# Layer 0 of a two-layer decoder: weight totals, scales, splits and ring loads half a section later, early loads issued by ScalarE, and another order of the last pair

## The chip, the cores and the metric

The kernel runs on one core of a Trainium2 chip. A core has a matrix engine (TensorE, in the profile PE, with its weight loads as PEld), VectorE (DVE), ScalarE (ACT), GpSimd (POOL) and SyncE (SP), which here does nothing but issue DMAs. Each engine works through its own list of instructions in order. The metric is the device time of one execution in microseconds (us); lower is better. Instructions and lines below (L427) are those of the kernel before.

## The reference

Two layers, each x + W_out(mixer(rmsnorm(x)) * silu(z)), on 1024 tokens of width 1024, 16 heads of 64. Layer 0 is forgetting attention, layer 1 a sparse attention that this change does not touch. Layer 0, cut:

```python
def fox_mixer(h, w_in, b_f, w_out):
    proj = h @ w_in
    q, k, v, f, z = jnp.split(proj, [W, 2 * W, 3 * W, 3 * W + N_HEADS], axis=-1)
    log_f = jax.nn.log_sigmoid(f.astype(jnp.float32) + b_f.astype(jnp.float32))
    c = jnp.cumsum(log_f, axis=1).transpose(0, 2, 1)
    for qb in range(S // FOX_BLOCK):
        logits = jnp.einsum('bqhd,bkhd->bhqk', q[:, s0:s1], k[:, :s1]) * scale
        logits = logits + c[:, :, s0:s1, None] - c[:, :, None, :s1]
        logits = jnp.where(tk[None, :] <= tq[:, None], logits, NEG)
        p = jax.nn.softmax(logits, axis=-1)
        outs.append(jnp.einsum('bhqk,bkhd->bqhd', p, v[:, :s1]))
    return (o * jax.nn.silu(z)) @ w_out
```

## The kernel before

Layer 0 works in 8 pairs of heads. For a pair, four **sections** are projected: k, v, q and z, 32 sections in all, each 128 columns of the weight. A section is two halves of 512 tokens, and a half is 8 steps over the width of 3 matmuls (L267 to L269): the weight and the activations are each split into two f16 parts, high and low, and three products of the parts are added.

A section's weight comes in as f32 by a DMA into a ring of 7 slots (`issue`, L413, tiles `wst_k`, `wst_v`, `wst_q`, `wst_z`). Before it is split, it is scaled by a power of two that is found from the sum of squares of the weight. For this `ring_square` (L421) squares it on ScalarE, five sections ahead, and adds up each row. Once a pair, when the squares of the next pair's four sections are there, `ring_total` casts the four row sums (`wtb`, L425, ScalarE) and adds them over the partitions with one matmul against ones (`wsum`, L427, PE). `ring_scale` (L436 to L441, VectorE) makes the scales from it in `wu`. Then `split_sec` splits the section: the high part on VectorE (L140, `whi_k` and so on), the low part on POOL (L144 and L145, `wlo_k` and so on), which overwrites the slot; a new ring load into that slot has to wait for it.

Between these sections the attention of earlier pairs runs, in units called **duos**: two tiles of 128 queries of one head. A duo's scores are matmuls S (L872 and L873); VectorE adds the bias and finds the minimum `m` (L881); ScalarE takes the exponential (L890) and a copy to f16 (`hl`, L891); VectorE makes the low part (L892); SP issues a DMA that transposes both parts (`pT`, L893); and PE multiplies by v (O, L905 to L907), two duos later. The bias needs `B`, a row of the cumulated forget gates that a DMA spreads over the partitions, and `Bd`, its diagonal block, made on POOL (L861).

A generator for the duos and one for the sections are merged by the planned cost of their matmuls, so that the program of PE alternates between them. What stands where on the other engines follows from the place at which a generator emits it. Each section calls `tick` twice: the first call behind its first half, the second behind its second. `next_w` keeps two split weights ready: called at a section's start, it emits the split of the section after it.

`early` squares further weights ahead of their use: rows of layer 0's output weight and 21 pieces of layer 1's input weight, 29 of up to 512 KB in all, one a section, by a load (L168) and a square on ScalarE (L174). `late_on` keeps an instruction at its place in program order. In the last pair the items are k, v, q, z, while the projections come as z half 1, q half 1, z half 0, q half 0, with a part of the output's work in between.

## Time and profile before

| | |
|---|---|
| median of 3 runs | 1470.51 us (1468.88 to 1470.97) |
| the profiled execution | 1472.43 us |
| its span on the core | 1470.7 us |
| PE busy | 1347.9 us (92%), 11084 matmuls |
| DVE, ACT, POOL busy | 1115.9, 933.7, 645.0 us |
| DMA | 234.79 MB, mean 160 GB/s |
| layer 0 | from about 40 to 600 us |

The profile is that of one execution; its own time is the span and what lies around it. Its second part shows the span in 40 slices of 36.8 us, in tenths, so the layer of interest is slices 2 to 16:

```profile
PE   5979989989998999999999988979999999998998
PEld 3435545555555555444545544446666666665643
DVE  6566677777777798496757666878998999889934
ACT  6666676776767674155455475657877878778512
POOL 0343546355454542221203456245765766755500
```

PE is the engine that is busy nearly throughout. A row of a timeline begins with its start and its duration in us; a bracket at the end tells how long the engine had been idle and what ended that. A view of waits tells who waited for whom, how long in all, how many times, and the longest.

### The profile page before, as it was taken

What the parts mean: (1) busy time and instruction counts of PE and PEld (TensorE: products, weight loads), DVE (VectorE), ACT (ScalarE), POOL (GpSimd) and SP (SyncE); (2) the same over time, 40 slices, a digit from 0 to 9 for tenths busy, and PEclk for the clock granted to TensorE, in tenths of its full rate; (3) what the DMA queues carried; (4) which work ended last, traced back from release to release, by engine and by line L of the source; (5) the groups of instructions that cost most, each with busy time, mean ns of one, the idle gap of its engine ahead of it and who ended that gap; (6) DMA issues with size and microseconds to landing.
All of it is one profiled execution on the core that took longest, in us unless ns stands there. A gap on an engine that the chain in (4) does not pass through costs nothing. (4 is left out here: it accounts for less than half of the span.)

```text
span 1470.7 us, 31545 instructions
## 1 busy us (share of the span) xinstructions
PE 1347.9 (92%) x11084; PEld 792.4 (54%) x11084; DVE 1115.9 (76%) x3005; ACT 933.7 (63%) x2291; POOL 645.0 (44%) x904
## 2 busy tenths in 40 slices
PE   5979989989998999999999988979999999998998
PEld 3435545555555555444545544446666666665643
DVE  6566677777777798496757666878998999889934
ACT  6666676776767674155455475657877878778512
POOL 0343546355454542221203456245765766755500
PEclk9999999999999999999999999999999999999999
DMA  7469789897798997446564547555667777776534
GB/s 271 105 155 196 178 158 219 169 202 189 172 213 174 200 203 178 107 155 201 154 206 125 151 111 161 123 145 89 127 144 155 146 170 128 143 156 147 107 108 143
DMA packets 410895, 234.79 MB, mean 160 GB/s; under 512 B 334000, under 2 KB 372208, under 8 KB 410736
## 3 DMA queue, kind: packets, MB, share of 16 engines
q1 hardware_dynamic: 410736, 232.78, 66.8%
q8 instruction: 87, 1.43, 0.4%
q14 instruction: 72, 0.59, 0.1%
HBM read 120.31 MB, written 28.38 MB: 101 GB/s over the span
## 5 line engine op out<-in xcount | busy, mean ns | idle before, releaser
L890 ACT ACTIVATE P<-P,m 128x512 f32<-128x512 f32 (+1 forms) x192 | 116.4, 607 | 111.6 <-DVE m L881 111.1
L1765 PE MATMUL S_n<-nk,nq 128*128 128x320 f16 (+5 forms) x768 | 154.5, 314 | 14.9 <-DVE m_n L1773 12.4
L1780 POOL TENSOR_TENSOR hl_n<-P_n,hl_n 128x640 f16<-128x640 f32 (+4 forms) x128 | 144.0, 1125 | 9.9
L892 DVE SCALAR_TENSOR_TENSOR hl<-P,hl 128x512 f16<-128x512 f32 (+1 forms) x192 | 120.6, 642 | 28.0 <-ACT hl L891 26.1
L861 POOL TENSOR_TENSOR Bd<-B,tri 128x128 f32<-128x128 f32 x128 | 65.2, 525 | 161.8 <-DVE m L881 129.8
L1779 POOL CAST hl_n<-P_n 128x640 f16<-128x640 f32 (+4 forms) x128 | 75.7, 592 | 125.8 <-ACT P_n L1776 107.2
L1776 ACT ACTIVATE P_n<-P_n,m_n 128x640 f32<-128x640 f32 (+7 forms) x128 | 98.6, 771 | 31.7 <-DVE m_n L1773 31.2
L1776 ACT ACTIVATE P_n<-P_n,m_n,units 128x640 f32<-128x640 f32 (+4 forms) x128 | 100.1, 782 | 21.6 <-DVE m_n L1775 20.3
L284 ACT ACTIVATE pth_n<-ptp_n 128x512 f16<-128x512 f32 (+1 forms) x160 | 85.1, 545 | 41.8 <-PE ptp_n L1798 41.3
L285 DVE SCALAR_TENSOR_TENSOR ptl_n<-ptp_n,pth_n 128x512 f16<-128x512 f32 (+1 forms) x160 | 99.6, 632 | 9.5 <-ACT pth_n L284 7.6
L1765 PEld LDWEIGHTS <-nq 128*128 128x128 f16 x768 | 71.5, 98 | 61.0 <-issue 25.7
L1798 PE MATMUL ptp_n<-ident,P_n 128*128 128x128 f32 x576 | 93.2, 280 | 8.0 <-DVE ptl_n L285 2.4
L891 ACT ACTIVATE hl<-P 128x512 f16<-128x512 f32 (+1 forms) x192 | 92.1, 512 | 6.0 <-DMA pT<-hl 4.1
L1773 DVE CUSTOM_DVE_ANT_0 P_n<-S_n,wmask 128x640 f32<-128x640 f32 (+4 forms) x128 | 83.2, 650 | 7.4 <-PE S_n L1765 6.9
L1798 PEld LDWEIGHTS ptp_n<-ident,P_n 128*128 128x128 f32 x576 | 65.3, 141 | 33.6 <-DVE ptl_n L285 7.1
L872 PE MATMUL S<-KH,Q 128*128 128x512 f32 (+1 forms) x192 | 76.5, 413 | 4.9 <-DVE wu L441 1.9
L97 ACT ACTIVATE h_n<-xr 128x512 f32<-128x512 f32 x32 | 20.0, 625 | 83.3 <-DVE xr L1898 41.0
L1806 PE MATMUL O_n<-nv,pth_n 128*128 128x64 f16 x576 | 71.7, 194 | 1.0 <-ACT pth_n L284 0.6
L1807 PE MATMUL O_n<-nv,pth_n 128*128 128x64 f16 x576 | 71.8, 193 | 0.0
L1773 DVE CUSTOM_DVE_ANT_0 P_n<-S_n,bias,units 128x640 f32<-128x640 f32 (+1 forms) x64 | 68.8, 1075 | 3.0 <-PE S_n L1765 2.9
L905 PE MATMUL O<-v,pT 128*128 128x64 f16 x576 | 59.6, 196 | 10.8 <-DMA pT<-hl 10.8
L1808 PE MATMUL O_n<-nv,ptl_n 128*128 128x64 f16 x576 | 68.8, 193 | 0.6 <-DVE ptl_n L285 0.6
(549 smaller groups left out, 4760.6 us busy)
## 6 DMA issues: line engine op xcount, KB each, us to landing
sq<-in_nsa_w_dram SPq DMA_DIRECT2D x28, 512.0 KB
B<-cD SPq DMA_DIRECT2D x16, 512.0 KB
nq<-qD SPq DMA_DIRECT2D x64, 128.0 KB
x<-in_x_dram SPq DMA_DIRECT2D x8, 512.0 KB
wst_k<-in_fox_w_dram SPq DMA_DIRECT2D x8, 512.0 KB
wst_v<-in_fox_w_dram SPq DMA_DIRECT2D x8, 512.0 KB
wst_q<-in_fox_w_dram SPq DMA_DIRECT2D x8, 512.0 KB
wst_z<-in_fox_w_dram SPq DMA_DIRECT2D x8, 512.0 KB
```

Source lines behind the costliest of these rows:

```text
L284: A.activation(hi[:, 0:n], pt[:, 0:n], AF.Copy, scale=scale)
L285: V.scalar_tensor_tensor(lo[:, 0:n], pt[:, 0:n], scale, h, OP.mult, OP.subtract)
L872: T.matmul(ps[:, 0:n], q, KH[j][:, k0:k0 + n], start=True, stop=False)
L890: A.activation(L[:, 0:n], L[:, 0:n], AF.Exp, bias=init, scale=-1.0, accum_out=self.lr[:, col + c:col + c + 1])
L891: A.activation(hi[:, cs], L[:, 0:n], AF.Copy, scale=UP)
L892: V.scalar_tensor_tensor(lo[:, cs], L[:, 0:n], UP, hi[:, cs], OP.mult, OP.subtract)
L1765: T.matmul(ps[:, b, 0:w], self.q[x][:, qi * P:(qi + 1) * P], k[:, k0 + b * w:k0 + b * w + w], start=(x == 0), stop=(x == 1))
L1773: V.tensor_tensor_reduce(dst, src, mk, 1.0 if y else unit, 3e38, OP.add, OP.min, m)
L1776: A.activation(L, L, AF.Exp, bias=m, scale=minus if y else -1.0, accum_out=self.l[:, y, qi:qi + 1])
L1779: G.tensor_copy(hl[:, 0:n], L)
L1780: G.tensor_tensor(hl[:, n:2 * n], L, hl[:, 0:n], OP.subtract)
L1798: T.transpose(pt[:, (x + i) * P:(x + i + 1) * P], L[:, kb * P - k0:(kb + 1) * P - k0], ident)
```

## The change

Three things move, all in layer 0; what is computed stays the same.

1. The pair total is emitted in the second tick of the q section instead of the first. Its scales, and the split of the next section, are emitted by a new function `prepare`, two steps into the second half of a section (for q of the last pair, which has no successor, not at all), instead of at the tick and at the next section's start. The ring's next load is issued in the second tick instead of the first.
2. The loads of `early` are issued by ScalarE, right behind the square that frees their buffer, instead of by SP in the second tick.
3. In the last pair the items, and so the loads and splits, come in the order k, v, z, q. The column of a section's scale is now found by its letter.

```diff
-                dma(t.rearrange("p (k c) -> p k c", k=k), src)
+                self.dma(t.rearrange("p (k c) -> p k c", k=k), src)
...
         def square(self):
             if self.at:
                 t, col = self.at.pop(0)
                 late_on(A.activation(t, t, AF.Square, accum_out=sums[:, col:col + 1]))
+            self.load()
...
-    items = [(a["fox_w"][kind * 8 + p], f"{x}{p}") for p in range(8) for x, kind in (("k", 1), ("v", 2), ("q", 0), ("z", 3))]
+    kinds = {"k": 1, "v": 2, "q": 0, "z": 3}
+    col = {"k": 0, "v": 1, "q": 2, "z": 3}
+    items = [(a["fox_w"][kinds[x] * 8 + p], f"{x}{p}") for p in range(8) for x in ("kvqz" if p < 7 else "kvzq")]
...
     def next_w():
-        while len(wq) < 2 and nsec[0] < 32:
+        if not wq:
+            prepare()
+        return wq.pop(0)
+
+    def prepare():
+        if totals:
+            ring_scale(*totals.pop())
+        if nsec[0] < 32:
             wq.append(split_sec(nsec[0]))
             nsec[0] += 1
-        return wq.pop(0)
+
+    def first_half(steps):
+        for i, c in enumerate(steps):
+            if i == 2:
+                prepare()
+            yield c
...
         if second:
             if n % 4 == 2 and n < 28:
-                ring_scale(n // 4 + 1, 0, 4, totals.pop())
-            early.load()
+                totals.append((n // 4 + 1, 0, 4, ring_total(n // 4 + 1, 0, 4)))
+            issue()
             sect[0] += 1
         else:
             if n + 5 < 32:
                 ring_square(n + 5)
             early.square()
-            issue()
-            if n % 4 == 2 and n < 28:
-                totals.append(ring_total(n // 4 + 1, 0, 4))
...
             pt = ps_a(f"v{p}_{half}")
-            yield from project(w, hT, half, pt)
+            steps = project(w, hT, half, pt)
+            yield from steps if half else first_half(steps)
...
             pt = ps_a(f"q{p}_{half}")
-            yield from project(w, hT, half, pt)
+            steps = project(w, hT, half, pt)
+            yield from first_half(steps) if half and p < 7 else steps
...
+    early.dma = lambda d, src: late_on(nc.scalar.dma_start(d, src))
...
-                ring_scale(0, 1, 4, pt)
+                totals.append((0, 1, 4, pt))
+                prepare()
...
-                wq, wz = next_w(), next_w()
+                wz = next_w()
                 yield from fox_z(p, wz, (1,))
-                yield from fox_q(p, wq, (1,))
+                w7 = next_w()
+                yield from fox_q(p, w7, (1,))
```

The sections k and z are changed in the same way as v and q. The rows below are the engines' own lists. The first place is ScalarE at the total for the fifth pair, the fourth of the seven (in the profile at 264): `wj` is a ring square, `sq` an early square, P and `hl` belong to a duo, Q is the cast of a projected half. Before:

```order
278 L421 ACTIVATE wj_3182,wu_107<-wst_z_2734 128x1024
279 L174 ACTIVATE sq_3028,sums<-sq_3028 128x1024
280 L425 CAST wtb_0_3187<-wu_107 128x4
281 L890 ACTIVATE P_1_2_1_0_3211,l_1_2_3206<-P_1_2_1_0_3211,m_1_2_1_3209 128x256
282 L890 ACTIVATE P_1_2_0_1_3224,l_1_2_3206<-P_1_2_0_1_3224,m_1_2_0_3222 128x384
283 L891 ACTIVATE hl_1_2_3204<-P_1_2_1_0_3211 128x256
284 L891 ACTIVATE hl_1_2_3204<-P_1_2_0_1_3224 128x384
285 L890 ACTIVATE P_1_2_0_0_3230,l_1_2_3206<-P_1_2_0_0_3230,m_1_2_0_3222 128x512
286 L656 ACTIVATE Q_0_0_3284<-q_0_3191,wu_106 64x512
```

And the same place of ScalarE in the changed kernel:

```order
292 L427 ACTIVATE wj_3182,wu_107<-wst_z_2815 128x1024
293 L174 ACTIVATE sq_2929,sums<-sq_2929 128x1024
294 L914 ACTIVATE P_1_2_1_0_3207,l_1_2_3202<-P_1_2_1_0_3207,m_1_2_1_3205 128x256
295 L710 DMA sq_3185<-in_nsa_w_dram 128x1024
296 L915 ACTIVATE hl_1_2_3200<-P_1_2_1_0_3207 128x256
297 L914 ACTIVATE P_1_2_0_1_3220,l_1_2_3202<-P_1_2_0_1_3220,m_1_2_0_3218 128x384
298 L914 ACTIVATE P_1_2_0_0_3226,l_1_2_3202<-P_1_2_0_0_3226,m_1_2_0_3218 128x512
299 L915 ACTIVATE hl_1_2_3200<-P_1_2_0_1_3220 128x384
300 L915 ACTIVATE hl_1_2_3200<-P_1_2_0_0_3226 128x512
301 L676 ACTIVATE Q_0_0_3280<-q_0_3187,wu_106 64x512
302 L431 CAST wtb_0_3286<-wu_107 128x4
```

The cast `wtb` has moved behind the next duo's exponentials and copies, the load's issue and the first Q cast. The second place is PE at the same total. Before, it stands among the projections of q:

```order
2744 L267 LDWEIGHTS whi_q_2817
2745 L267 MATMUL q_0_3191<-hT_0_101,whi_q_2817 128x512
2746 L427 LDWEIGHTS ones
2747 L427 MATMUL wsum_0_3189<-wtb_0_3187,ones 128x4
2748 L268 LDWEIGHTS whi_q_2817
2749 L268 MATMUL q_0_3191<-hT_0_101,whi_q_2817 128x512
```

In the changed kernel it stands behind the end of q, a part of z and the S of the next duo:

```order
2820 L270 LDWEIGHTS wlo_z_3083
2821 L270 MATMUL z_1_3293<-hT_1_102,wlo_z_3083 128x512
2822 L896 MATMUL S_1_3_1_0_3309<-KH_1_1748,Q_0_1_2400 128x128
2823 L897 MATMUL S_1_3_1_0_3309<-KL_1_1750,Q_0_1_2400 128x128
2824 L896 MATMUL S_1_3_0_1_3321<-KH_1_1748,Q_1_1_2297 128x512
2825 L897 MATMUL S_1_3_0_1_3321<-KL_1_1750,Q_1_1_2297 128x512
2826 L896 MATMUL S_1_3_0_0_3327<-KH_1_1748,Q_1_1_2297 128x512
2827 L433 LDWEIGHTS ones
2828 L433 MATMUL wsum_0_3288<-wtb_0_3286,ones 128x4
```

It has moved by 11 projection matmuls, 27 of O and 5 of S. The third place is SP at the first duos of the first pair, with the row `B`, the transposes of v and pT, the ring's `wst` and the early `sq`. Before:

```order
39 L644 DMA_TRANSPOSE v_523<-vs_1_598 128x8x128
40 L845 DMA B_0_717<-cD 128x1024
41 L845 DMA B_1_1026<-cD 128x1024
42 L168 DMA sq_698<-in_fox_w_out_dram 128x1024
43 L893 DMA_TRANSPOSE pT_0_0_720<-hl_0_0_719 128x8x128
44 L413 DMA wst_z_1083<-in_fox_w_dram 128x1024
45 L893 DMA_TRANSPOSE pT_0_0_720<-hl_0_0_719 128x10x128
46 L893 DMA_TRANSPOSE pT_0_1_768<-hl_0_1_767 128x6x128
47 L893 DMA_TRANSPOSE pT_0_1_768<-hl_0_1_767 128x12x128
```

SP in the changed kernel:

```order
36 L869 DMA B_0_701<-cD 128x1024
37 L663 DMA_TRANSPOSE v_512<-vs_0_594 128x8x128
38 L663 DMA_TRANSPOSE v_512<-vs_1_598 128x8x128
39 L869 DMA B_1_1026<-cD 128x1024
40 L917 DMA_TRANSPOSE pT_0_0_704<-hl_0_0_703 128x8x128
41 L917 DMA_TRANSPOSE pT_0_0_704<-hl_0_0_703 128x10x128
42 L917 DMA_TRANSPOSE pT_0_1_768<-hl_0_1_767 128x6x128
43 L917 DMA_TRANSPOSE pT_0_1_768<-hl_0_1_767 128x12x128
44 L416 DMA wst_z_1186<-in_fox_w_dram 128x1024
```

The first `B` has moved ahead of the transposes of v, `wst_z` behind four transposes of pT, and `sq` is no longer there.

More of the change, by code (lines that the diff above doesn't have):

```diff
@@ L158, in __init__ @@
         def __init__(self, pool, items, size, bufs, tag="sq"):
-            self.tag = tag
+            self.tag, self.dma = tag, dma
             self.pool, self.items, self.size, self.bufs, self.at = pool, items, size, bufs, []
@@ L415, in tile_fox_nsa, with sec_col @@
     wu = [hp.tile([P, 18], F32, name=f"wu{p}") for p in range(8)]
+    def sec_col(n):
+        return col[items[n][1][0]]
     def ring_square(n):
         j = sa.tile([P, D], BF16, tag="sq", bufs=1, name=f"wj_{n}")
-        late_on(A.activation(j, ring[n].rearrange("p k c -> p (k c)"), AF.Square, accum_out=wu[n // 4][:, n % 4:n % 4 + 1]))
+        late_on(A.activation(j, ring[n].rearrange("p k c -> p (k c)"), AF.Square, accum_out=wu[n // 4][:, sec_col(n):sec_col(n) + 1]))
     def ring_total(p, x, y):
@@ L445, in split_sec @@
         parts = [wp.tile([P, KC, P], F16, tag=f"w{x}", bufs=2, name=f"w{x}_{name}") for x in ("hi", "lo")]
-        return split_w16(ring[n], wu[n // 4][:, 5 + n % 4:6 + n % 4], parts, n > 0)
+        return split_w16(ring[n], wu[n // 4][:, 5 + sec_col(n):6 + sec_col(n)], parts, n > 0)
     wq, nsec = [], [1]
     def next_w():
-        while len(wq) < 2 and nsec[0] < 32:
+        if not wq:
[5 more added lines that the diff above has]
+        if nsec[0] < 32:
             wq.append(split_sec(nsec[0]))
             nsec[0] += 1
-        return wq.pop(0)
+    def first_half(steps):
[3 more added lines that the diff above has]
+            yield c
     gain0, sect = [], [0]
@@ L536, in fox_k @@
             pt = ps_a(f"k{p}_{half}")
-            yield from project(w, hT, half, pt)
+            steps = project(w, hT, half, pt)
+            yield from steps if half or not p else first_half(steps)
             if p and half == 0:
@@ L650, in fox_q @@
             pt = ps_a(f"q{p}_{half}")
-            yield from project(w, hT, half, pt)
+            steps = project(w, hT, half, pt)
+            yield from first_half(steps) if half and p < 7 else steps
             for j in range(2):
@@ L669, in fox_z @@
             pt = ps_a(f"z{p}_{half}")
-            yield from project(w, hT, half, pt)
+            steps = project(w, hT, half, pt)
+            yield from first_half(steps) if half else steps
             zs[half] = z = sb[0].tile([P, 512], F32, tag="z", bufs=4, name=f"z_{p}_{half}")
@@ L725, in fox_fill @@
             else:
-                wq, wz = next_w(), next_w()
+                wz = next_w()
                 yield from fox_z(p, wz, (1,))
-                yield from fox_q(p, wq, (1,))
+                w7 = next_w()
+                yield from fox_q(p, w7, (1,))
                 rows0 = conv_wout(1, 200, 2)
                 yield from fox_z(p, wz, (0,))
-                last_q = fox_q(p, wq, (0,))
+                last_q = fox_q(p, w7, (0,))
                 for _ in range(2):
```

## The prediction

> **What bounds the kernel now.** The change touches layer 0 alone, so the first view is the busy time of each engine in stretches of layer 0: us, then PE, PEld, DVE, ACT and POOL busy with instruction counts, granted clock, DMA share, GB/s.
>
> ```profile
> 60.00:110.00 50.00, 39.59 (x237) 20.19 (x237) 30.31 (x96) 31.10 (x73) 23.50 (x38) 0.94 0.63 151
> ...
> 180.00:240.00 60.00, 54.96 (x422) 30.62 (x421) 45.42 (x147) 42.95 (x104) 30.90 (x50) 0.97 0.89 190
> 240.00:300.00 60.00, 56.63 (x430) 32.03 (x429) 46.70 (x149) 43.16 (x105) 26.92 (x47) 0.97 0.88 181
> 300.00:360.00 60.00, 56.04 (x445) 31.35 (x444) 45.46 (x144) 44.20 (x108) 27.07 (x45) 0.94 0.86 193
> 360.00:430.00 70.00, 66.75 (x512) 37.94 (x510) 52.95 (x166) 48.37 (x117) 38.62 (x64) 1.00 0.87 195
> 430.00:490.00 60.00, 55.22 (x444) 31.42 (x443) 44.79 (x145) 41.75 (x104) 28.81 (x50) 0.97 0.88 183
> ```
>
> PE is busy for 92 to 95% of every stretch after 180; the others leave a quarter or more free. So in layer 0 the time is PE's work, plus PE's gaps, plus what half clock adds. The gaps, from the view of waits of PE between 60 and 640 (who waits for whom: us, times, longest):
>
> ```profile
> PE wsum L427 <- ACT wtb L425: 19.6, 7, 4.7
> PE O L905 <- DMA pT<-hl: 10.8, 4, 4.1
> ...
> PE S L872 <- DVE wu L441: 1.9, 1, 1.9
> ...
> PE z L269 <- POOL wlo_z L145: 1.3, 1, 1.3
> ```
>
> The largest is the pair total: a matmul of 0.16 us that waits for ScalarE's small cast `wtb`. One of the seven, in the timelines of PE and then of ACT (start, us, instruction, in brackets the idle time before and its cause):
>
> ```profile
> 198.58 0.40 PE L873 MATMUL S<-KL,Q 128*128 128x512 f32 x1
> 203.63 0.16 PE L427 MATMUL wsum<-wtb,ones 128*128 128x4 bf16 x1 [4.65 <-ACT wtb L425]
> ...
> 204.03 0.63 PE L268 MATMUL q<-hT,whi_q 128*128 128x512 f16 x1
> 204.46 0.63 PE L269 MATMUL q<-hT,wlo_q 128*128 128x512 f16 x1
> ...
> 206.71 0.38 PE L269 MATMUL z<-hT,wlo_z 128*128 128x512 f16 x1
> 206.92 0.38 PE L267 MATMUL z<-hT,whi_z 128*128 128x512 f16 x1
> ...
> 207.57 0.19 PE L905 MATMUL O<-v,pT 128*128 128x64 f16 x1
> ...
> 208.35 0.38 PE L267 MATMUL z<-hT,whi_z 128*128 128x512 f16 x1
> ```
>
> ```profile
> 202.36 1.04 ACT L174 ACTIVATE sq<-sq 128x1024 f32<-128x1024 f32 x1
> ...
> 203.40 0.18 ACT L425 CAST wtb<-wu 128x4 bf16<-128x4 f32 x1
> 203.48 0.40 ACT L890 ACTIVATE P<-P,m 128x128 f32<-128x128 f32 x1
> ...
> 204.00 0.31 ACT L891 ACTIVATE hl<-P 128x128 f16<-128x128 f32 x1
> 206.41 0.68 ACT L656 ACTIVATE Q<-q,wu 64x512 fp32r<-64x512 f32 x1 [2.10 <-PE q L269]
> 207.00 0.71 ACT L890 ACTIVATE P<-P,m 128x512 f32<-128x512 f32 x1
> ...
> 208.41 1.14 ACT L891 ACTIVATE hl<-P 128x512 f16<-128x512 f32 x2
> ```
>
> The cast stands behind a square of 1.04 us, so it ends at 203.6, when PE has waited 4.65 us. Behind the stall the projection matmuls start every 0.43 us (204.03, 204.46) instead of every 0.21 (206.71, 206.92): half clock, until about 206.2. That loss is read from the granted clock: 3% of 60, 3% of 60, 6% of 60 and 3% of 60 us make 9.0 us in the four stretches from 180 with a clock under 1.00; 360 to 430, with a total's stall of its own, shows none.
>
> **The change part by part.** All sums are against the profiled execution, 1472.43 us (span 1470.7), 1.9 above the median of 1470.51; I take 1.9 off at the end.
>
> *Pair totals.* In program order the matmul moves behind some 6 projection matmuls of q, 13 of z and 27 of O at 198.98: 19 x 0.215 + 0.78 (207.57 to 208.35) = 4.9 us, so PE arrives at 203.9. But the cast moves too: it now stands behind the next duo's exponentials, the load's issue and the first Q cast. From the rows above: 203.4 + 0.8 (203.48 to 204.31) + the issue, say 0.54 + 2.55 (207.00 to 209.55) + 0.68 + 0.18 = 208.1, since Q need no longer wait its 2.10 us for a stalled PE. The stall is then 4.2 instead of 4.65. The next total, and what stands around it:
>
> ```profile
> 264.10 0.18 ACT L425 CAST wtb<-wu 128x4 bf16<-128x4 f32 x1
> ...
> 268.04 0.68 ACT L656 ACTIVATE Q<-q,wu 64x512 fp32r<-64x512 f32 x1 [1.25 <-PE q L269]
> ```
>
> The cast moves to 268.04 - 1.25 + 0.68 + 0.54 + 0.62 for one more cast ahead of Q = 268.6, by 4.5 us; PE comes 4.7 later (11 projections, 27 O, 5 S). The last four of the seven totals, of PE:
>
> ```profile
> 264.32 0.16 PE L427 MATMUL wsum<-wtb,ones 128*128 128x4 bf16 x1 [3.37 <-ACT wtb L425]
> ...
> 327.82 0.16 PE L427 MATMUL wsum<-wtb,ones 128*128 128x4 bf16 x1 [3.96 <-ACT wtb L425]
> ...
> 388.77 0.16 PE L427 MATMUL wsum<-wtb,ones 128*128 128x4 bf16 x1 [3.25 <-ACT wtb L425]
> ...
> 449.44 0.16 PE L427 MATMUL wsum<-wtb,ones 128*128 128x4 bf16 x1 [3.85 <-ACT wtb L425]
> ```
>
> The wait of 3.37 becomes 3.2, or with PE's rows at full clock some 2.8. The sixth and seventh move in the same way, PE by about half a us more than the fourth (three more projections each), so I put them at 2.4 and 2.8. At the fifth the cast stays, and PE comes later by three projections and an S, 1 us: 2.9. The five together, 15.1 for 19.1: **gain 4 us** of the 19.1 that all five hold; ends 0 (cast and matmul move alike) and 19.1 (ACT is early everywhere).
>
> *Half clock.* A stall of 3.25 us (the one in 360 to 430) drew no half clock, one of 3.37 did. If four of the five stalls fall under 3, only the first keeps its dip (1.8): 7.2 us would go. I take **4**, half of it, as the gaps of other kinds remain and may join; ends 0 and 9.0. The Trainium skill (TensorE: Matmul & The Clock Gate, Part 1: The HAM clock gate) says that the rate halves after an idle window of about 3.4 us, on a free-running grid. The trace agrees with the size, by 3.25 and 3.37; by that rule alone the term would be the whole 7.2.
>
> *Scales, split and ring issue.* Five small VectorE operations and a split of 0.75 us leave the chain of the duo at the pair's end and stand in a later one. VectorE is 75% busy and does them either way. At the first pair it shows (PE, then SP):
>
> ```profile
> 78.25 0.41 PE L872 MATMUL S<-KH,Q 128*128 128x384 f32 x1 [1.92 <-DVE wu L441]
> 90.13 0.20 PE L905 MATMUL O<-v,pT 128*128 128x64 f16 x1 [3.70 <-DMA pT<-hl]
> ...
> 108.97 0.23 PE L905 MATMUL O<-v,pT 128*128 128x64 f16 x1 [4.06 <-DMA pT<-hl]
> ```
>
> ```profile
> 84.79 0.33 SPq L413 DMA_DIRECT2D wst_z<-in_fox_w_dram x1
> 85.22 5.00 SPq L893 DMA_TRANSPOSE pT<-hl x3
> ```
>
> ```profile
> 82.11 0.69 DVE L892 SCALAR_TENSOR_TENSOR hl<-P,hl 128x512 f16<-128x512 f32 x1
> ```
>
> Before, the second transpose of the first duo stands behind `wst_z` on SP; afterwards that load stands behind four transposes. So 1.92 goes with the scales, and about 2.4 of the 3.70 (the transpose can be issued at 82.8, when VectorE's row ends, instead of 85.22), with some of the 3.0 of half clock (6% of 50 us). The third gap has the same chain of exponentials behind it, and PE arrives earlier: it may take back up to all of this. Ends +2 (taken back, with a dip) and -7; I take **gain 3**. Elsewhere the ring's loads move by one or two places on SP and keep over a section until their square; 0.
>
> *Early loads on ScalarE.* Twenty-nine issues leave SP. The instructions of that line on SP (duration min/median/max, times):
>
> ```profile
> L168 SPq DMA_DIRECT2D sq<-in_nsa_w_dram x20: 327/538/1631, 168.9 to 469.9; - x20
> L168 SPq DMA_DIRECT2D sq<-in_fox_w_out_dram x7: 333/691/1100, 62.1 to 155.2; - x7
> ```
>
> On ScalarE 29 x 0.54 = 16 us are to be placed. The group of exponentials there shows the cover (busy, mean ns, idle before and its cause, 60 to 560):
>
> ```profile
> L890 ACT ACTIVATE P<-P,m 128x512 f32<-128x512 f32 (+3 forms) x174 | 105.5, 607 | 89.0 <-DVE m L881 88.7
> ```
>
> 89 us of idle time wait for VectorE's minima, so most of 16 us falls into idle time. What shows is 0.54 in front of four totals, counted already, and a little at the transposes: **cost 1**. If the cover is gone, it is 16; if relieved SP passes transposes earlier, -3. What SP gains sits on no chain PE waits for, but for the first pair.
>
> *Last pair.* With z split ahead of q, the wait of z for `wlo_z`, **1.3**, goes; q's split ends as much ahead of q as z's did behind z. Ends 0 and 1.3.
>
> Sum: -4 - 4 - 3 + 1 - 1.3 = -11.3, that is 1461.1 for the profiled execution, **1459** for a median.
>
> **The rivals.** *All the totals' stalls go.* ScalarE is late because it also waits for PE and VectorE (the 2.10 before Q); with PE not stopped, its queue may run ahead and the cast be there in time. Then -19.1 - 9.0 - 3 - 1.3 = -32: 1438. Against it: the cast moves behind five or six operations. *Only moved.* Cast and matmul go later by the same amount (4.5 and 4.7 at the fourth), and what PE saves there returns at the next `pT`, whose transposes come from the same late chain: within 3 us, 1468 to 1473. This is also the case in which the change does not do what it says: half a section in program order is no half section of slack. *Slower.* The load's issue on ScalarE takes the length of one of SP's transposes (5.00 for three at 85.22, 1.7 each) on top of 0.54, because both issue at once. It then stands in the chain from square to exponential: four totals come 1.7 later (+7), the half clock stays, and the same 1.7 at some four of the transposes without slack adds another 5, less 1.3 and 3 for the other parts: +8, 1478. It decides from an issue of about 1.5 us, where the gain of 4 at the totals and of 4 in the clock is used up. SP's own longest row, 1631 ns, says that such an issue can occur; the median of 538 speaks against. The Trainium skill (Perfetto Trace Analysis, DMA Instruction — HWDGE) says that the block which makes the descriptors is shared between issuing engines and locked for one at a time, the lock's wait being part of the shown duration. By that page the 1.7 us would be met wherever SP is inside a transpose; no trace of this kernel shows ScalarE issuing, so it cannot be tested here yet, and it is why this rival has the chance that it has.
>
> **How the numbers follow.** Forecast (-6 to -17: 1454 to 1465) 0.45; all stalls gone (1436 to 1453) 0.17; only moved 0.22; slower (1474 to 1485) 0.16. Leaving out half of the second case and over half of the last gives a range of 1442 to 1477. About 0.2%, 3 us, is what a measurement of this kernel can tell from no change: faster 0.62, same 0.22, slower 0.16.
>
> **What would show it.** Right: waits of `wsum` for `wtb` of some 15 us in five places, 2 to 4 each; the granted clock at 0.98 or more from 240 to 490; no S that waits for `wu` and a shorter first wait for `pT`; ScalarE's issues near 0.5 us; no z that waits for `wlo_z`. Wrong: issues of over 1.5 us on ScalarE; a new group of PE waits for `pT` beyond 11 us; a wait of ScalarE's square for its own load; q of the last pair waiting for `wlo_q`; waits of `wsum` near zero (then it is the first rival).

## The result, and the profile after

| | before | changed |
|---|---|---|
| median of 10 runs each | 1470.74 us (1466.65 to 1476.36) | 1477.63 us (1474.57 to 1487.44) |
| ratio of the changed kernel, 95% interval | | 1.0056 (1.0037 to 1.0074) |
| the profiled execution, its span | 1472.43, 1470.7 us | 1478.88, 1476.9 us |

The changed kernel is slower by 0.56%, about 8 us, where some 11 us less were forecast. The view of stretches shows that most of layer 0 did what the forecast wanted (columns as before):

```profile
60.00:110.00 50.00, 42.58 (x264) 22.71 (x265) 32.97 (x115) 34.87 (x82) 23.90 (x40) 0.93 0.73 169
180.00:240.00 60.00, 57.52 (x466) 32.87 (x464) 45.21 (x151) 43.15 (x107) 31.32 (x51) 1.00 0.93 196
240.00:300.00 60.00, 57.38 (x458) 32.34 (x458) 45.95 (x147) 45.94 (x110) 31.07 (x51) 1.00 0.88 198
300.00:360.00 60.00, 56.36 (x446) 31.45 (x442) 46.31 (x150) 43.45 (x108) 31.13 (x52) 1.00 0.94 200
360.00:430.00 70.00, 64.31 (x493) 35.88 (x492) 47.80 (x152) 48.81 (x118) 30.32 (x52) 1.00 0.85 184
430.00:490.00 60.00, 48.65 (x376) 26.68 (x374) 41.94 (x140) 35.62 (x88) 25.97 (x43) 0.89 0.86 148
```

From 180 to 430 the granted clock is 1.00 throughout, where before it dipped in three of four stretches. The last row breaks with that: PE is busy for 48.65 us instead of 55.22, at a clock of 0.89. PE's waits from 60 to 640:

```profile
PE O L929 <- DMA pT<-hl: 24.6, 10, 8.1
PE wsum L433 <- ACT wtb L431: 9.3, 5, 2.6
```

The totals' waits halve, 19.6 to 9.3 us. The waits for transposes `pT` more than double, 10.8 to 24.6, and one alone takes 8.1 us. The start of each section's first projection on PE says where that falls. The table has the lead over the kernel before in us, one profiled execution each; the starts before are 116.59, 206.17, 454.50, 469.46 and 519.74, those of the changed kernel 110.17, 198.58, 445.50, 472.00 and 522.80. The experiments below are entered already:

| lead at | v, 2nd pair | z, 3rd | z, 7th | k, last | last q |
|---|---|---|---|---|---|
| changed | 6.4 | 7.6 | 9.0 | -2.5 | -3.1 |
| changed, again (e1) | 6.6 | 8.9 | 11.6 | 1.8 | 0.9 |
| changed, loads on SP (e2) | 4.2 | 8.0 | 11.9 | 10.2 | 10.9 |
| before, loads on ScalarE (e3) | 3.2 | 0.9 | -12.9 | -14.7 | -15.9 |
| before, half a section later (e7) | 4.5 | 7.0 | 9.8 | 8.3 | 8.3 |
| changed, ring behind pT (e17) | 14.7 | 13.6 | 27.7 | 23.6 | 25.3 |

The changed kernel is ahead by 9.0 us until z of the seventh pair and loses 11.5 within that one section. The timeline of PE there shows the loss as a gap, with matmuls at half rate behind it (459.08 to 459.49):

```profile
448.52 0.16 PE L433 MATMUL wsum<-wtb,ones 128*128 128x4 bf16 x1 [1.12 <-ACT wtb L431]
...
457.65 0.23 PE L929 MATMUL O<-v,pT 128*128 128x64 f16 x1 [8.08 <-DMA pT<-hl]
...
459.08 0.61 PE L268 MATMUL z<-hT,whi_z 128*128 128x512 f16 x1
459.49 0.63 PE L269 MATMUL z<-hT,whi_z 128*128 128x512 f16 x1
```

The clock's records have three windows of 3.41 us at half clock one behind the other from 451.56, some 5 us more. The queue of SP, and ScalarE's:

```profile
437.17 0.33 SPq L416 DMA_DIRECT2D wst_o<-in_fox_w_out_dram  x1
437.59 3.48 SPq L663 DMA_TRANSPOSE v<-vs  x2
441.24 1.17 SPq L917 DMA_TRANSPOSE pT<-hl  x1
442.50 0.53 SPq L869 DMA_DIRECT2D B<-cD  x1
443.12 16.95 SPq L917 DMA_TRANSPOSE pT<-hl  x4
```

```profile
443.93 0.33 ACTq L710 DMA_DIRECT2D sq<-in_nsa_w_dram  x1
...
457.68 0.52 ACT L915 ACTIVATE hl<-P 128x384 f16<-128x384 f32 x1 [9.20 <-issue]
```

ScalarE issues its load while SP is inside the transposes. What the DMA engines did in 449 to 457, the stretch of the gap:

```profile
DMA packets 1741, 0.93 MB, mean 117 GB/s; under 512 B 1612, under 2 KB 1612, under 8 KB 1740
...
q1 hardware_dynamic: 1596, 0.40, 77.7%
q10 hardware_dynamic: 144, 0.52, 45.0%
```

q1 is SP's queue, q10 ScalarE's. The same 8 us of the kernel before, where both kinds of transfer come from SP's queue:

```profile
DMA packets 3155, 1.79 MB, mean 224 GB/s; under 512 B 2898, under 2 KB 2898, under 8 KB 3154
```

Half the bytes move in the same time, and nearly all packets are the small ones of transposes, for which PE waits. (ScalarE's own 9.20 us end 0.03 us behind PE's, most likely with the same transposes, since its copy needs the buffer that they read; the profile names no releaser.)

The load isn't the whole of it. Its first packet moves only at 449.11, and from 445 to 448, with no packet of q10, SP's own transposes beside the row `B` are slow too:

```profile
DMA packets 567, 0.31 MB, mean 102 GB/s; under 512 B 527, under 2 KB 527, under 8 KB 566
```

A second gap in front of `pT` stands at the first pair, PE and SP:

```profile
103.51 0.23 PE L929 MATMUL O<-v,pT 128*128 128x64 f16 x1 [6.95 <-DMA pT<-hl]
```

```profile
94.12 0.33 SPq L416 DMA_DIRECT2D wst_k<-in_fox_w_dram  x1
94.55 1.19 SPq L917 DMA_TRANSPOSE pT<-hl  x1
```

SP had nothing to issue from 87.8 to 94.12, because the ring load `wst_k`, whose slot POOL's split of v had not yet released, stood ahead of the third duo's transposes. This gap has another cause than the first: the runs below with the loads on SP have it too (6.22 us in e2, 5.82 in e7), so it comes with part 1 and not with part 2.

### The profile page after: what moved, and what is told of

Read it like the earlier page. It is cut to its first block, busy times and chain, and to the rows that moved or that the text cites. A ratio compares the mean times of both kernels' runs of the same rounds, so it can differ in the third digit from the quotient of the medians.

```text
span 1476.9 us, 31543 instructions
## 1 busy us (share of the span) xinstructions
PE 1348.5 (91%) x11084; PEld 790.9 (54%) x11084; DVE 1110.6 (75%) x3005; ACT 932.8 (63%) x2291; POOL 646.5 (44%) x904
## 5 line engine op out<-in xcount | busy, mean ns | idle before, releaser
L1789 PE MATMUL S_n<-nk,nq 128*128 128x320 f16 (+5 forms) x768 | 154.4, 314 | 14.7 <-DVE m_n L1797 12.2
L916 DVE SCALAR_TENSOR_TENSOR hl<-P,hl 128x512 f16<-128x512 f32 (+1 forms) x192 | 116.2, 622 | 41.5 <-ACT hl L915 39.4
L1800 ACT ACTIVATE P_n<-P_n,m_n,units 128x640 f32<-128x640 f32 (+4 forms) x128 | 100.1, 782 | 21.9 <-DVE m_n L1799 20.7
L929 PE MATMUL O<-v,pT 128*128 128x64 f16 x576 | 58.5, 195 | 26.9 <-DMA pT<-hl 24.6
L929 PEld LDWEIGHTS <-pT 128*128 128x128 f16 x576 | 52.1, 99 | 38.6 <-DMA pT<-hl 32.8
```

The costliest lines, as they stand in the source:

```text
L916: V.scalar_tensor_tensor(lo[:, cs], L[:, 0:n], UP, hi[:, cs], OP.mult, OP.subtract)
L929: T.matmul(o, self.hT[:, b0 + k, :], vk[:, 0], start=(k == 0 and u == 0), stop=False)
L1789: T.matmul(ps[:, b, 0:w], self.q[x][:, qi * P:(qi + 1) * P], k[:, k0 + b * w:k0 + b * w + w], start=(x == 0), stop=(x == 1))
L1800: A.activation(L, L, AF.Exp, bias=m, scale=minus if y else -1.0, accum_out=self.l[:, y, qi:qi + 1])
```

## The experiments

The letters are those of the expectations. Theory A: the loads themselves cost the time, once they leave SP's queue and run beside the transposes on the same DMA engines. Theory B: the half-section moves lengthen the chain of ScalarE and VectorE. Theory C: chance, one late instruction in that one execution. Theory D, from e12 on: what costs is that the order of SP's queue changes, so that ring loads or rows stand ahead of transposes. To these comes theory E: ScalarE itself is held up, by its issues or by instructions that come late. Ratios are to the kernel before, measured side by side with the run.

| run | median us | ratio (95%) |
|---|---|---|
| e1 changed again | 1474.75 | one execution |
| e2 changed, loads on SP | 1463.04 | 0.9960 (0.9945 to 0.9975) |
| e3 before, loads on ScalarE behind the square | 1491.26 | 1.0159 (1.0146 to 1.0173) |
| e4 changed, ScalarE's loads in the second tick | 1458.26 | 0.9931 (0.9918 to 0.9944) |
| e5 changed, half of each load | 1464.52 | 0.9960 (0.9944 to 0.9975) |
| e6 before, ScalarE's loads in the second tick | 1468.10 | 0.9988 (0.9967 to 1.0009) |
| e7 before, half a section later only | 1460.95 | 0.9945 (0.9926 to 0.9964) |
| e10 as e4, total's matmul later | 1465.55 | 0.9992 (0.9973 to 1.0010) |
| e11 before, ScalarE loads an eighth | 1466.60 | 0.9989 (0.9971 to 1.0007) |
| e12 changed, SP in program order | 1522.39 | 1.0355 (1.0328 to 1.0382) |
| e13 as e12, loads in the second tick | 1520.22 | 1.0346 (1.0314 to 1.0379) |
| e14 as e3, SP in program order | 1517.03 | 1.0328 (1.0297 to 1.0359) |
| e15 as e12, loads on SP | 1498.78 | 1.0200 (1.0175 to 1.0225) |
| e16 as e2, total's matmul later | 1459.90 | 0.9931 (0.9914 to 0.9948) |
| e17 changed, ring loads behind pT on SP | 1447.01 | 0.9843 (0.9823 to 0.9863) |
| e18 as e17, loads in the second tick | 1456.26 | 0.9904 (0.9885 to 0.9923) |

### One part at a time: e1, e2, e3, e7

e1 is the changed kernel unedited.

> The changed kernel once more, unchanged, for a second profile. Theory A (the loads on ScalarE's queue mix with SP's transposes on the same DMA engines, and the worst mix comes each time at the same place): the 8.1 us gap of PE near 449 us, with a load of some 7.6 us there, is seen again, time 1475 to 1485. Theory B (the half-section moves lengthen the chain of ScalarE and VectorE): no such single gap, many small waits, time about 1477. Theory C (chance: one late instruction fetch of ScalarE in that one execution): no gap over 5 us near 449, the time about 1475 or below.

The gaps come again at the same places, 7.10 us at 96.46 and 4.31 at 448.52, the second at about half its length; so they belong to the kernel, and theory C falls. e2 takes part 2 out of the changed kernel, e3 puts it alone into the kernel before; e7 is e2 with the last pair as before, so part 1 alone.

```diff
 e2, against the changed kernel
-            self.load()
...
+            early.load()
...
-    early.dma = lambda d, src: late_on(nc.scalar.dma_start(d, src))
 e3, against the kernel before
+            self.load()
...
-            early.load()
...
+    early.dma = lambda d, src: late_on(nc.scalar.dma_start(d, src))
```

> The changed kernel with part 2 undone: the early loads are issued by SP in the second tick again, half-section moves and last pair kept. Theory A: the long gap near 449 and the one near 96 go; 1457 to 1464, ratio to before about 0.993. Theory B: as the changed kernel, 1475 to 1480, ratio 1.005. Theory C: about 1470 to 1476, since nothing of the cause depends on the queue.

> The kernel before with part 2 alone: the early loads issued by ScalarE behind the square. Theory A: slower than before by 8 to 18 us (1478 to 1488), with a wait of O for pT of over 5 us in at least one place and loads of over 5 us there. Theory B: same as before, 1467 to 1473. Theory C: same as before within 3 us in most executions.

> The kernel before with part 1 alone (totals, scales, split and ring half a section later), loads on SP, last pair as before. From the changed kernel with its loads on SP (1463.0) less the last pair's 1.3: 1463 to 1466, ratio about 0.997; if the last pair were the whole gain, 1467.

Part 1 alone gains 0.55%, parts 1 and 3 together 0.40%, with intervals that overlap: part 3 gains nothing that shows, and e7 is 2 us faster than expected. Part 2 alone costs 1.6%, and about 1% on top of the others (1.0056 against 0.9960, not measured side by side; the one execution of e1 against e2, side by side, gives 11.7 us, 0.8%). That is the whole of the result's sign, and theory B falls with it: the half-section moves alone make the kernel faster. The expectation of e2 that the gap near 96 would go as well was a miss; the one near 449 went. e3 came out 3 us above the range expected of theory A, and none of its waits for `pT` is over 5 us. PE's waits for `pT` of e2, then of e3:

```profile
PE O L928 <- DMA pT<-hl: 11.7, 6, 6.2
```

```profile
PE O L906 <- DMA pT<-hl: 23.7, 10, 4.5
```

With the loads on SP the waits stay at the level of before (10.8); with the loads on ScalarE they double, in either kernel.

At the gap of the seventh pair e2 and the changed kernel can be laid side by side. From 437.17 to 468 SP's list has the same rows in the same order in the changed kernel, in e2 and in the kernel before, the early load aside. This is the third transpose of `pT` behind the row `B`, in the changed kernel, where the load runs beside it, and in e2, where the load stands two rows ahead of it in the same queue:

```profile
449.92 7.53 SPq L917 DMA_TRANSPOSE pT<-hl  x1
```

```profile
445.77 2.60 SPq L916 DMA_TRANSPOSE pT<-hl  x1
```

The first transpose behind `B` is drawn out in both, 5.21 us and 4.44, so `B` alone doesn't make the gap: in e2 the next ones are quick again, PE doesn't wait for `pT` there at all, and from 444 to 452 the DMA engines move 213 GB/s. At this place, then, SP's order is not the cause, and the load on the second queue is. In e3 the cost is spread over several places. Two of its waits (3.84 us until 289.63 and 2.90 until 418.61) stand where a load for the ring or the output weight has moved ahead of a transpose, so there the loads and the order aren't separated.

### The same loads at another moment: e4, e6

The load stays on ScalarE and moves from the square to the second tick, half a section later (e4 in the changed kernel, e6 in that of before):

```diff
-            self.load()
...
+            early.load()
```

> The changed kernel with the early loads on ScalarE still, but issued in the second tick, about half a section later. Theory A: the worst mix goes to another place or is milder: 1462 to 1482, and where a PE gap over 5 us is left, a load and transposes overlap there. Theory B: as the changed kernel, 1475 to 1480. Theory C: as the changed kernel.

> The kernel before with the loads on ScalarE in the second tick, nothing else changed. Theory A says that the time depends on where loads meet transposes: better than the 1491 of the loads behind the square, 1462 to 1478. If ScalarE's queue were harmful wherever the load stands, it would be near 1485 to 1492.

Half a section is worth 1.2% in the changed kernel and 1.7% in the one before; e4 came out even below the range expected of theory A. So ScalarE as the issuer isn't the cost, nor its 29 issues, and theory E falls. Neither run is clean. In e4 the cast `wtb` also comes to stand right behind the square. And SP's order moved with the loads: of its more than 800 rows besides the early loads, at least 14 stand elsewhere in e3 than in the kernel before but only 4 in e6, and e4 differs from the changed kernel in at least 11. So these two don't set A apart from D. e6's profiled execution was its longest run (1479.89), so its trace is not used as a measure.

### Fewer bytes: e5, e11

e5 loads half of each piece in the changed kernel and squares it twice; e11 loads an eighth in the kernel before and squares it eight times. Both therefore scale the weights that `early` squares by other sums.

```diff
 e5 (e11 alike: 8, 128 and 0:1)
+                h = t.shape[1] // 2
+                src = t[:, 0:h][:, None, :].to_broadcast([P, 2, h]) if self.cut else t
...
+            d, src = d[:, 0:4], src[:, 0:4]
+        late_on(nc.scalar.dma_start(d, src))
```

> The changed kernel, but each early load brings half of its 512 KB (the square reads that half twice, so ScalarE's time stays; the sums of squares behind the scales differ from the reference's). Theory A (the loads on a second queue mix with the transposes): with half the bytes the wait of O for pT falls from 22 to 25 us to under 17, the long gap near 449 to under 4, time 1462 to 1469. If the queue alone or the place of the instruction on ScalarE were the cause, and not the bytes: 1473 to 1480, waits as in the changed kernel.

> The kernel before with the loads on ScalarE behind the square, which took 1491, but each brings an eighth of its bytes (the square reads them eight times over, so the sums of squares differ from the reference's). Theory A (the bytes that mix with the transposes): 1462 to 1472. If the instruction's place or the moved order of SP were the cause: 1484 to 1492.

With half the bytes 1.0056 becomes 0.9960, the value of e2; with an eighth 1.0159 becomes 0.9989. In e11 the waits for `pT` are those of before:

```profile
PE O L917 <- DMA pT<-hl: 9.7, 4, 3.8
```

This is what A predicts. It isn't proof: smaller loads also moved at least 6 (e5, against the changed kernel) and 11 (e11, against e3) of SP's rows to other places, and e11's order is within 4 rows of that of the kernel before. At the gap of the seventh pair, though, e5's list is that of the changed kernel row for row, and there PE waits only 0.7 us for `pT`; the three transposes behind `B` take 3.92, 3.43 and 2.02 us.

### The transfers by themselves: e8, e9

Behind the end of the kernel, when all else is done, e8 and e9 add sets of transposes (four and eight of them) with a 512 KB load, issued by SP between them (F) or by ScalarE: in e8 together with the transposes, in e9 (M) once the first has landed.

> The kernel before with a tail of 20 pieces behind the output, each ended by small VectorE operations that wait for all of it, in the order T, L, F, A, B, four times. T: four transposes of 128x2048 on SP alone. L: one load of 512 KB on ScalarE's queue alone. F: load, then the four transposes, all on SP. A: load on ScalarE and the four transposes on SP at once. B: the same, with the load behind the first transpose. Theory A: A and B take longer than T and L together, by 1 us or more (from the trace some 1.4 us of transposes and 2.3 of a load took 7.6 when mixed), and longer than F. If mixing is harmless, A and B take no longer than F, and the packets of the transposes are as short as in T.

> As the tail of the last look, with eight transposes and a load that starts in their midst: T eight transposes on SP alone; L a load on ScalarE alone; F the load on SP behind the second transpose; M the load on ScalarE, which waits until the first transpose has landed, so that its packets come while SP goes on issuing. Theory A: M takes over 1 us longer than F, the issue of a transpose beside the load grows from 2.3 to over 4 us, and the load from 2.1 to over 4. If mixing only shares the engines: M ends with F within 0.5 us.

In e8 the load, issued together with the transposes, hardly ran among them (some 60 to 240 of their packets fall between its own); from the first issue to the last read the sets with a load took 13.2 to 13.8 us in either form, which tells nothing. In e9 they mix a little more. Its instructions, F and then M, and the DMA view of M from 1540.9 to 1545, from the load's issue to its landing:

```profile
1511.95 4.54 SPq L1936 DMA_TRANSPOSE bdst<-bsrc  x2
1516.58 0.81 SPq L1932 DMA_DIRECT2D bload<-in_nsa_w_dram  x1
...
1535.88 0.15 DVE L1925 CAST bx<-bdst 128x1 f32<-128x1 f16 x1 [2.16 <-DMA bdst<-bsrc]
...
1536.37 21.06 SPq L1936 DMA_TRANSPOSE bdst<-bsrc  x8
...
1541.07 0.35 ACTq L1932 DMA_DIRECT2D bload<-in_nsa_w_dram  x1
...
1559.62 0.15 DVE L1925 CAST bx<-bdst 128x1 f32<-128x1 f16 x1 [2.19 <-DMA bdst<-bsrc]
```

```profile
DMA packets 1886, 0.96 MB, mean 235 GB/s; under 512 B 1758, under 2 KB 1758, under 8 KB 1886
```

F takes 23.9 us from its first issue (1511.95) to the read of its last transpose; M, counted from 1536.37, takes 23.25. The other three of each take 23.3 to 23.4 and 23.0 to 23.3, eight transposes alone 21.7 to 21.9. The row of the transpose next to the load shows 4.30 us instead of some 2.3, and the set as a whole loses nothing: 235 GB/s, not 117. So a load among transposes is not always a loss, and A as it was put misses here. But the tail doesn't repeat what happens at 449: the load is through in 2.0 us, as when it is alone (2.0 to 2.3), with some 280 of the transposes' packets between its own, where in the changed kernel it takes 7.6 us with over 1300.

### A later matmul for the total: e10, e16

The total's matmul is split from its cast and put two steps into the next section, the scales to step 5; e10 builds on e4, e16 on e2.

```diff
+    def ring_sum(p, x, y, tb):
...
+                if totals:
+                    add_up()
+                    late = 5
```

> The kernel with the loads on ScalarE in the second tick (1458.3 beside 1467.5 before), and the total's matmul apart from its cast: the cast in the second tick, the matmul two steps into the next section, scales and split at step five. The wait of wsum for wtb, 7.3 us there, falls under 2; time 1450 to 1458, unless the later scales make k wait for its split (then 1460 or more).

> The changed kernel with the loads on SP (1463 beside 1467.5 before) and the total's matmul apart from its cast, two steps into the next section, scales and split at step five. With the loads off ScalarE's queue the wait of O for pT stays under 12 us (60 to 560) and the wait of wsum falls from 11.6 to under 3: 1450 to 1458. If what wsum gives up returns as waits for pT, as it did with the loads on ScalarE (18.1 us there): 1460 to 1466.

PE's waits in e10:

```profile
PE O L945 <- DMA pT<-hl: 20.7, 9, 7.4
...
PE wsum L435 <- ACT wtb L430: 1.1, 1, 1.1
```

The totals' stall can be taken away nearly whole, 7.3 to 1.1 us; part of it then comes back at `pT` (17.3 in e4, 20.7 here, in an execution 5 us faster than e10's median), and the kernel is slower than e4 (0.9992 against 0.9931). With the loads on SP the same step helps a little at most (0.9931 against e2's 0.9960, intervals that touch), and there too the waits for `pT` rise, from 11.7 to 15.6 us. Neither pair was measured side by side, and both runs miss the 1450 to 1458 that was expected.

### The order on SP: e12 to e15, e17, e18

To test D, SP's order has to stand still while the loads move. e12 to e15 hold it in program order for ring loads, rows B and the transposes of v and pT alike:

```diff
-            dma(ring[-1], src)
+            late_on(dma(ring[-1], src))
...
-                dma(b, cD[2 * p + j:2 * p + j + 1, :].to_broadcast([P, S]))
+                late_on(dma(b, cD[2 * p + j:2 * p + j + 1, :].to_broadcast([P, S])))
```

> The changed kernel with SP's ring loads, rows B and transposes kept in the order in which the program emits them, so that a ring load, which waits for POOL's split, no longer stands in front of the transposes of the same duo. Loads on ScalarE behind the square as in the change. Theory A (the loads' bytes on the second queue at that place): little changes, 1474 to 1482. Theory D (with the early loads off SP, the scheduler puts the ring loads one place ahead of the transposes, and SP blocks on the split): the loss goes, 1455 to 1465.

> As the one before, with the same order of ring loads, B and transposes on SP, but the early loads on ScalarE in the second tick. Theory A: faster than its partner by 10 us or more, since only the loads' place differs. Theory D: within 4 us of its partner.

> The kernel before with the loads on ScalarE behind the square (1491 in the look with the scheduler's order), and SP's ring loads, B and transposes in program order. Theory A: 1483 to 1494. Theory D: 1463 to 1473.

> The changed kernel with the loads on SP in the second tick and the same three kinds of SP instructions in program order. Theory A and theory D both say near 1455 to 1465; as a control it shows what the order of SP alone does beside the 1463 of its partner with the scheduler's order.

All four are slower by 2 to 3.6%, for a reason of their own. The largest wait of PE in e12:

```profile
PE S L896 <- DVE m L905: 62.7, 16, 6.8
```

The rows B now come too late for VectorE's bias (from 60 to 560 it waits 61.1 us for them), and PE waits there; for `pT` it waits 1.0 us in all. Of what was expected only one thing came, theory D's for e13: it is within 4 us of e12, and the two have all the held rows in the same order. But as PE waits elsewhere, this says little about loads beside transposes; e15 is faster than e12, but its held rows stand in another order in at least 18 of 195 places. For A against D these four are inconclusive. e17 and e18 hold only the ring loads and the transposes of pT, and leave B free; the loads stay on ScalarE, behind the square in e17, in the second tick in e18.

```diff
-            dma(ring[-1], src)
+            late_on(dma(ring[-1], src))
...
-            nc.sync.dma_start_transpose(self.hT[:, b0:b0 + 2 * nk, :], self.hl[:, b0 * P:(b0 + 2 * nk) * P])
+            late_on(nc.sync.dma_start_transpose(self.hT[:, b0:b0 + 2 * nk, :], self.hl[:, b0 * P:(b0 + 2 * nk) * P]))
```

> The changed kernel with only ring loads and pT transposes kept in program order on SP (rows B and v free to move, since they were what made the last four slow). Loads on ScalarE behind the square. If the bytes at that place cost: its wait of O for pT is 5 us or more above its partner's, and it is 5 us or more slower. If the order of ring loads and transposes on SP was the cause: both within 4 us, and near 1460.

> The partner of the one before: the same order kept on SP, the loads on ScalarE in the second tick. Expectations as there.

e17 is the fastest of all, 1.6% ahead of the kernel before, and holds all three parts of the change as they were; part 2 is at the very place at which it cost 1.6% in e3. Its waits, SP's queue at the first pair, and its stretches:

```profile
PE wsum L433 <- ACT wtb L431: 7.8, 5, 2.7
PE O L929 <- DMA pT<-hl: 6.5, 3, 3.4
```

```profile
89.95 6.98 SPq L917 DMA_TRANSPOSE pT<-hl  x4
96.97 1.30 SPq L416 DMA_DIRECT2D wst_q<-in_fox_w_dram  x1
```

```profile
60.00:110.00 50.00, 49.27 (x329) 26.26 (x328) 40.28 (x135) 39.83 (x95) 29.40 (x50) 1.00 0.82 177
...
430.00:490.00 60.00, 58.99 (x464) 33.65 (x463) 45.37 (x149) 39.64 (x104) 32.93 (x52) 0.97 0.93 190
```

At the first pair SP goes on with transposes while the ring load waits behind them; the gap of 6.95 us and its half clock are gone, which is 49.27 us of PE work in the first stretch for 42.58. Loads still meet transposes in e17, and slowly: from 118 to 127 the DMA view shows

```profile
DMA packets 1401, 0.97 MB, mean 108 GB/s; under 512 B 1242, under 2 KB 1242, under 8 KB 1400
...
q10 hardware_dynamic: 144, 0.52, 36.3%
```

and yet PE's only gap from 116 to 130 is this one, behind a cast:

```profile
128.80 0.16 PE L433 MATMUL wsum<-wtb,ones 128*128 128x4 bf16 x1 [1.07 <-ACT wtb L431]
```

So the slow meeting costs nothing where the transposes have room. e17's list differs from the changed kernel's in at least 30 rows, most of them ring loads, which stand later through the whole of layer 0. Neither expectation came: e17 is not slower than its partner e18 by 5 us, nor within 4 of it, but 9 us faster (0.9843 against 0.9904, measured side by side), with 6.5 us of waits for `pT` against 11.2; 9 of SP's other rows differ between the two.

Neither theory stands alone. For A speaks the gap of the seventh pair, where SP's order is that of e2 and only the load's queue differs, and where half the bytes leave a wait of 0.7 us. For D speaks that e17 and the changed kernel have the same loads at the same place on ScalarE and differ in SP's order alone, by 2% of the time (1.0056 against 0.9843). e3 against e6 and e11 fits both. What fits all the runs is that loads beside transposes can draw these out, and that the order on SP decides whether PE is waiting for just those. The last link is argued from the traces; e17's order with the loads on SP, which would give the price of the loads in it, wasn't run.

## Why the prediction was wrong

Point by point, with the forecast in brackets:

- **Pair totals** (gain 4): the direction held and the size was better. The waits fell by 10.3 us, 19.6 to 9.3. The example of 203.63 waits 1.91 us instead of 4.65, where 4.2 were worked out:

```profile
204.25 0.16 PE L433 MATMUL wsum<-wtb,ones 128*128 128x4 bf16 x1 [1.91 <-ACT wtb L431]
```

  Counted from the start of that q section, PE's arrival moved by 4.7 us, near the 4.9 worked out, but the cast only by 2.0 instead of 4.5, because ScalarE's square ahead of it came 2.2 us sooner. e10 and e16 then show that such a gain need not stay: with the stall gone or nearly gone, part of it returns at `pT`. That was the rival "only moved".
- **Half clock** (gain 4): the dips of 180 to 360 went, as the term wanted. At 451 a run of three windows came with the new gap. The whole span has 20 windows of half clock, where it had 19, so on the whole this term brought nothing.
- **First pair** (gain 3): no S waits for `wu` any more, and PE is busy for 42.58 us instead of 39.59 in the first stretch, 3.0 more; the three gaps of 9.68 us became one of 6.95. Right, but not for the whole reason given: a ring load (`wst_k`) that stands ahead of transposes keeps most of the gap. The same gap stands in e7 (5.82 us), where no load is on ScalarE.
- **Parts 1 and 3** together (sum -12.3): e2 measures -0.40%, 6 us; part 1 alone -0.55%, 8 us. The sign was right, the sum about twice what came for both and over a third too large for part 1 (-11 worked out).
- **Last pair** (gain 1.3): z no longer waits for `wlo_z`, as said; no gain is to be seen in the time (e2 against e7).
- **Early loads on ScalarE** (cost 1): this is the step that failed. "On ScalarE 29 x 0.54 = 16 us are to be placed" priced the issue, and the issue is cheaper still:

```profile
L710 ACTq DMA_DIRECT2D sq<-in_nsa_w_dram x20: 334/335/361, 159.8 to 469.4; - x20
L710 ACTq DMA_DIRECT2D sq<-in_fox_w_out_dram x8: 334/335/398, 43.9 to 149.1; - x8
```

  What the step left out is the transfer. In SP's queue a load of 512 KB was served in its turn between transposes; from a second queue it can run beside them, and at 449 a transpose that takes 2.60 us in e2 took 7.53, while PE waited 8.08 us for `pT`. "What SP gains sits on no chain PE waits for" looked at SP's time only; the chain from `hl` over the transposes to O runs through the same DMA engines. And "Elsewhere the ring's loads move by one or two places on SP and keep over a section until their square; 0" looked at the squares that wait for the loads, and not at the transposes behind them: taking 29 issues out of SP's list changed the places of at least 13 others (e2's list against the changed kernel's), and e17 shows what such places can be worth: 2% of the kernel (1.0056 against 0.9843). In place of a cost of 1 the runs show some 14 us on top of the other parts (12 by e1 against e2), 23 us alone. How much of that is the transfer and how much the order is settled only for the seventh pair, by e2. The sign named ahead for this, a group of PE waits for `pT` beyond 11 us, came: 24.6, of which 6.95 at the first pair belong to part 1.
- **The slower rival** had the direction and another mechanism. It wanted issues of 1.5 us or more on ScalarE; the longest is 0.398 us, and e4, e6 and e17 have the same issues without the loss. Its sum, besides, counts 1.7 us at four transposes as 5, where 6.8 would make it 1480.
- **A reading**: VectorE leaves 22 to 25% of the stretches from 180 free, not a quarter or more; no term rests on that.

Of the 14 us on top of the other parts, 9.8 have a place: from z of the seventh pair to k of the last the changed kernel loses 11.5 us of its lead and e2 1.7. That is the gap of 8.08 us with three windows of half clock behind it (some 5 us), where e2 has one. Another 2.9 stand ahead of that section and 1.3 between it and the last q. The changed kernel's span is longer than that before by 6.2 us, and 3.1 of these arise behind the last q, mostly in layer 1's unchanged instructions (a lead of -3.1 there, -6.2 at the end); e2 loses 3.7 there as well, so this is not part 2's. Where the windows of half clock fall differs there between the traces; that this is the cause wasn't tested.

What stays open: why a load among transposes makes the DMA engines so slow in the kernel (7.6 us for the load that begins to move at 449.11, 117 GB/s) and not in the tail (e9, 235 GB/s). Four loads take over 5 us in the changed kernel and e17 together, and within 7 us of three of them a row B, 512 KB spread over the partitions, was issued (442.50 above); it wasn't tried alone. The other 27 loads of 512 KB in the changed kernel take 1.3 to 5.2 us, so one meeting in 28 made most of the loss. Which of the rows that e17 moves on SP bring its gain, beyond those of the first pair, was not taken apart either. One thing in the words on the change has to be read otherwise: `prepare` runs two steps into the first half of a section, not into its second. So the totals and the ring's loads move by half a section, the splits by two steps only, and the scales from the second tick of q to two steps into z; the terms above were worked out from the engines' lists and don't rest on that.

## What to carry to other kernels

A DMA that is moved to another engine's queue is not only an issue that moves: it leaves its turn in a FIFO and competes with what it used to follow, so its price is read from the transfers that it will run beside, and from who waits for those. When instructions are taken out of a queue whose order a scheduler makes, compare the whole new order; look for a load with a late release that stands ahead of transfers the matrix engine needs. And a stall that is removed upstream has to be followed to the next wait: here part of it came back at `pT` (e10, e16).

## What the runs showed of the hardware

- ScalarE's issue shows 0.33 us at 443.93, while SP is in its four transposes from 443.12; the load's first packet moves 5.2 us later, at 449.11. Where a load runs alone, in e9, it moves 1.0 us after the issue. The Trainium skill (Perfetto Trace Analysis, DMA Instruction — HWDGE) counts the wait for the shared block into the shown duration. No such wait shows in any of the 29 rows here (334 to 398 ns), so the delay has to be read from the packets.
- The Trainium skill (DMA: Bandwidth & Descriptors, Issuing engines are not separate DMA queues) says that DMAs from different engines share the same 16 DMA engines and that issuing from several saves only the issue. The trace agrees with the first half: q1 and q10 move packets in the same 8 us. The second half leaves out a cost that the seventh pair shows: with the load on the second queue 117 GB/s moved in the 8 us of the gap, and a transpose took 7.53 us, where it took 2.60 in e2.
- Behind the kernel's end, one load from the second queue among eight transposes cost no more than one in their own queue (23.25 against 23.9 us), though the row of the transpose next to it took 4.30 us instead of some 2.3.
